# Down projection of a gated conv FFN on one core: where the raw weight rows of the seven-product units lie, which queue loads them, and how many such units there are

## The chip, the cores and the metric

The kernel runs on one core of one Trainium2 chip. The metric is the device time of one execution in microseconds (us). Each time given is a median of a few executions. The trace of before is one more execution of the same kernel, recorded by the hardware profiler.

## The reference

One decoder layer on 256 tokens with a model width of 2048: a mixer of two attention branches, then a gated feed-forward network. Only the last part of the second one matters here, the down projection of a [256, 5632] activation with a [5632, 2048] float32 matrix, followed by a norm with the scale `norm_ffn_post` and the residual sum.

```python
def conv_ffn(h, w_up, conv_w, conv_b, w_down):
    a, b = jnp.split(h @ w_up, 2, axis=-1)
    ...
    return (jax.nn.gelu(c, approximate=True) * b) @ w_down

h = rms_norm(x, norm_ffn_pre[l])
y = conv_ffn(h, ffn_w_up[l], ffn_conv_w[l], ffn_conv_b[l], ffn_w_down[l])
x = x + rms_norm(y, norm_ffn_post[l])
```

## The kernel before

All weights are float32 in DRAM. A chunk of 128 rows by 1024 columns (512 KB) comes into a **raw** tile. ScalarE rounds it to a high half `whi`, VectorE subtracts to get the low half `wlo` (`convert`, lines 143 and 144), and TensorE multiplies in three passes (`mm3`, lines 175 to 177: high weights, low weights, then high weights with the low half of the activation). The raw tiles are a ring of three (`RAW = 3`), the pairs of halves a ring of four and one more; a load is issued on SyncE's queue as soon as its raw tile has been read by both engines, and SyncE takes its loads strictly in order.

The 5632 columns of the activation are made in eleven groups of 512 (`ffn_up(c, ...)`, c = 0 to 10, lines 1041 and 1045). Each group leaves two evacuation tiles, tags `fa` and `fb` with two buffers each, which the convolution and the gating (`conv_cols`, lines 930 to 938) read. After group 5 the first 24 tiles of 128 columns (k = 0 to 23) are complete, and `down_pair(p)` multiplies them with their rows of `w_down`: p = 0 for output columns 0 to 1023, p = 1 for columns 1024 to 2047. Then come groups 6 to 10 and the rest of the down projection.

`down_pair` walks over 12 **units** of two row tiles each, of two kinds:

- `plain(u)`: two rows of weights through SyncE and the raw ring, each multiplied with both token tiles and both halves of the columns, 2 x 4 products of three passes: 24 matmuls.
- `seven(u)`: the two rows `even` and `odd` and the two token tiles are taken as a 2 x 2 block product, done with seven products instead of eight: 21 matmuls. VectorE forms four sums of weights (`ta`, `tb`, lines 1124 to 1127, in tiles of the tags `fa` and `fb`); `odd`, half of `even`, `ta` and `tb` are converted, in this order. The sums of the activation (`s_of`) were made earlier, for units 0 to 3.

In the text a unit of seven products is called a seven, and the sevens are numbered through both passes. `PAIR_ORDER` writes out the order of the units: `psppsppsppsp`, the same for both p, so there are 2 x 4 sevens and 2 x 8 plain units. The products use all eight PSUM banks, four named `c` and four named `q`; the two sets change places between p = 0 and p = 1. After the last seven of a pass VectorE and ScalarE empty `q` into `ds` (lines 1141 to 1145), after the last unit `c` (line 1155). After p = 1 the next group's product `ua` writes into the banks that were `q`.

`gpost2` is the tile with the scale `norm_ffn_post`, 1 MB for 128 partitions. It uses the one buffer of tag `gp`, is loaded on GpSimd's queue before group 1, and is read first after group 10. Between, GpSimd's queue only writes the residual stream to DRAM (`park`, line 1007). It is read back on SyncE's queue (`unpark`, line 1013) into tiles that the token sums `s` hold before.

Inside `trunk_layer` a scheduler puts the instructions of each engine into a fixed order when the program is built; each engine then runs its list in that order and waits on semaphores.

Of the kernel before, what the change touches and what calls it, by code (L numbers as in the profile page):

```python
# [19 lines left out]
P = 128  # L20
D = 2048
# [20 lines left out]
def trunk_layer(ctx, tc, x, x_cols_in, conv_cols_in, g_mix_post, g_ffn_post, w_in, w_q, w_kv,  # L42
                sinks, rel, wo_a, wo_b, w_out, w_up, w_down, rope_tab, strip_sel, out):
    nc = tc.nc
    vec, act, pe, pool = nc.vector, nc.scalar, nc.tensor, nc.gpsimd

    def open_pool(name, bufs=1, **kw):
        es = ExitStack()
        return es, es.enter_context(tc.tile_pool(name=name, bufs=bufs, **kw))
# [9 lines left out]
    def sb(pl, shape, name, dt=F32, tag=None, bufs=None):  # L59
        return pl.tile(shape, dt, name=name, tag=tag or name, **({"bufs": bufs} if bufs else {}))  # L60
# [46 lines left out]
    def ring_tile(kind, name, dt, extra):  # L107
        pl_tag = dict(name=name, tag="flex", bufs=2) if extra else dict(name=name, tag=kind, bufs=RAW if kind == "raw" else RING)
        return ring.tile([P, 1024], dt, **pl_tag)

    def in_turn(kind):

        turn[kind] += 1
        return flex[0] == kind and turn[kind] % (RAW + 2 if kind == "raw" else RING + 1) >= (RAW if kind == "raw" else RING)
# [19 lines left out]
    def convert(raw, n, own=None, parts=None):  # L134
        i = cnt[0]
        cnt[0] += 1
        if own:
            hi, lo = (own.tile([P, 1024], F32R, name=f"w{part}{i}", tag="w" + part) for part in ("hi", "lo"))
        else:
            extra = in_turn("w")  # L140
            hi, lo = (ring_tile("w" + part, f"w{part}{i}", F32R, extra) for part in ("hi", "lo"))
        for a, b in parts or ((0, n),):
            act.copy(hi[:, a:b], raw[:, a:b])  # L143
            vec.tensor_tensor(lo[:, a:b], raw[:, a:b], hi[:, a:b].bitcast(F32), op=ALU.subtract)  # L144
        return hi, lo

    def raw_row(src):
        i = cnt[0]
        cnt[0] += 1
        raw = ring_tile("raw", f"raw{i}", F32, in_turn("raw"))  # L150
        nc.sync.dma_start(raw, src)
        return raw
# [4 lines left out]
    def at(t, *fs):  # L157
        steps[max(t, now[0])].extend(fs)

    def tick():  # L160
        for f in steps.pop(now[0], ()):
            f()
        now[0] += 1
# [10 lines left out]
    def mm3(o, ah, al, bh, bl, start, stop):  # L174
        pe.matmul(o, ah, bh, start=start, stop=False)  # L175
        pe.matmul(o, ah, bl, start=False, stop=False)  # L176
        pe.matmul(o, al, bh, start=False, stop=stop)  # L177

    def gemm(xh, xl, w, k0, nk, c0, n, split=None, extra=None, ps=None):

        kc = 1024 // n if n in (256, 512) else 2
        acc = new_acc("g", ps)
        todo = []
        cuts = list(range(0, nk, kc)) + [nk]
        for ci, (k, ke) in enumerate(zip(cuts[:-1], cuts[1:])):
            kk = ke - k
            src = w[(k0 + k) * P:(k0 + k + kk) * P, c0:c0 + n].rearrange("(a p) n -> p a n", p=P)
            hi, lo = wchunk(src, [kk, n], *(extra or {}).get(ci, ()))
            for j in range(kk):
                kt = k + j  # L190
                wh, wl = hi[:, j * n:(j + 1) * n], lo[:, j * n:(j + 1) * n]
                for t in range(NT):
                    x_ = [x(k0 + kt)[:, t * P:(t + 1) * P] for x in (xh, xl)]
                    if split is None or t == 0 or ci < split:
                        mm3(acc[t][:, :n], *x_, wh, wl, kt == 0, kt == (split * kc if split and t else nk) - 1)
                    else:
                        todo.append((kt, x_, wh, wl))
            tick()
        return acc, todo
# [377 lines left out]
    acc, _ = gemm(XH, XL, w_in, 0, KT, 0, 512)  # L577
# [4 lines left out]
    acc, _ = gemm(XH, XL, w_in, 0, KT, C_KV, KVR + ROPE)  # L582
# [201 lines left out]
    for j in range(4):  # L784
        acc, _ = gemm(XH, XL, w_in, 0, KT, C_GA + 512 * j, 512)
# [15 lines left out]
    es6, p6 = open_pool("p6")  # L801
# [33 lines left out]
    for j in range(4):  # L835
        ld = merge_loads(j)
        acc, _ = gemm(AH, AL, wo_a, 0, KT, 512 * j, 512)
# [60 lines left out]
    for b in range(4):  # L898
        c0, n = W_BLOCKS[b]
# [109 lines left out]
    def unpark(t, j):  # L1009
        if j == 0:  # L1010
            x2_all[t] = sb(p3, [P, D], f"x2b_{t}", tag=f"x2_{t}")
        c = slice(j * 512, (j + 1) * 512)
        nc.sync.dma_start(x2_all[t][:, c], x2_d[t, :, c])
# [59 lines left out]
            at(now[0] + 1 + 2 * i, lambda i=i: conv_cols(4 * c + i, sa[0][i], sa[1][i], slot0 + i))  # L1073

    es7 = ffn_up0()
    gpost2 = sb(p6, [P, D], "gpost2", tag="gp")
    pool.dma_start(gpost2, g_ffn_post.partition_broadcast(P))
    for c in range(1, 6):
        if c == 2:
            for i in range(8):  # L1080
# [11 lines left out]
    def banks(kind, name):  # L1092
        return [(pacc if kind == 0 else (pss, pst)[i // 2]).tile([P, 512], F32, name=f"{name}{i}", tag="acc" if kind == 0 else "st"[i // 2])
                for i in range(4)]

    def down_pair(p):

        c11, c12, c21, c22 = c = banks(p, f"c{p}_")
        q1, q5, q7, q6 = q = banks(1 - p, f"q{p}_")
        j0, used = 2 * p, set()  # L1100
        d = [dsum[t][j0 + j] for t in range(NT) for j in range(2)]
        act_of = lambda k, t: (GH(k)[:, t * P:(t + 1) * P], GL(k)[:, t * P:(t + 1) * P])
        row = lambda k: w_down[k * P:(k + 1) * P, j0 * 512:(j0 + 2) * 512]
        half = lambda w, i: tuple(x[:, i * 512:(i + 1) * 512] for x in w)

        def mul(o, x, w, last=False):
            mm3(o, *x, *w, id(o) not in used, last)
            used.add(id(o))

        def plain(u, last):  # L1110
            for k in (2 * u, 2 * u + 1):
                w = convert(raw_row(row(k)), 1024)
                for t in range(NT):
                    for j in range(2):
                        mul(c[2 * t + j], act_of(k, t), half(w, j), last and k % 2 == 1)
                tick()

        def seven(u, last):
            s1, s2, s3, s4 = s_of[u]
            even, odd = raw_row(row(2 * u)), raw_row(row(2 * u + 1))  # L1120
            ta, tb = (sb(p6, [P, 1024], f"t{n}{p}_{u}", tag="f" + n, bufs=2) for n in "ab")
            lo_, hi_ = slice(0, 512), slice(512, 1024)
            w = convert(odd, 1024)
            vec.tensor_tensor(ta[:, lo_], even[:, hi_], even[:, lo_], op=ALU.subtract)
            vec.tensor_tensor(ta[:, hi_], odd[:, hi_], even[:, hi_], op=ALU.subtract)
            vec.tensor_tensor(tb[:, lo_], odd[:, hi_], ta[:, lo_], op=ALU.subtract)
            vec.tensor_tensor(tb[:, hi_], odd[:, lo_], tb[:, lo_], op=ALU.subtract)
            mul(c11, act_of(2 * u + 1, 0), half(w, 0))
            mul(c12, s4, half(w, 1))
            w = convert(even, 512)  # L1130
            mul(q1, act_of(2 * u, 0), half(w, 0), last)
            w = convert(ta, 1024)
            mul(q5, s1, half(w, 0), last)
            mul(q7, s3, half(w, 1), last)
            tick()
            w = convert(tb, 1024)
            mul(q6, s2, half(w, 0), last)
            mul(c21, act_of(2 * u + 1, 1), half(w, 1))
            tick()
            if last:  # L1140
                act.copy(d[0], q1)
                vec.tensor_tensor(d[1], d[0], q6, op=ALU.add)
                vec.tensor_tensor(d[2], d[1], q7, op=ALU.add)
                vec.tensor_tensor(d[3], d[2], q5, op=ALU.add)
                vec.tensor_tensor(d[1], d[1], q5, op=ALU.add)  # L1145

        plain_of, seven_of = iter(range(4, 12)), iter(range(4))
        for i, kind in enumerate(PAIR_ORDER):
            if kind == "s":
                u = next(seven_of)  # L1150
                seven(u, u == 3)
            else:
                plain(next(plain_of), i == len(PAIR_ORDER) - 1)
        for o, x in zip(d, c):
            vec.tensor_tensor(o, o, x, op=ALU.add)

    for p in range(2):
        down_pair(p)
    for i in range(8):
        at(now[0] + 40 + 2 * i, lambda i=i: unpark(i // 4, i % 4))  # L1160
    for c in range(6, 11):
# [65 lines left out]


RING = 4
PAIR_ORDER = "psppsppsppsp"  # L1230
XCUT = [0, 1, 2, 3, 4, 6, 8, 10, 12, 14, 16]
X_LOAD = [0, 1, 2, 3, 4, 6, 7, 8, 10]
X_SQ = [4, 4, 5, 5, 6, 7, 8, 9, 10, 11]
# [71 lines left out]
```

## Time and profile before

| what | value |
|---|---|
| median of 3 runs | 1474.38 us (1473.21 to 1476.98) |
| the profiled execution | 1475.35 us |
| its span, from the first to the last instruction | 1473.5 us |
| TensorE busy | 1460.6 us, 99% of the span |
| VectorE, ScalarE busy | 1026.6 us (70%), 818.3 us (56%) |
| GpSimd busy | 51.1 us (3%) |
| DMA | 287.58 MB, 195 GB/s in the mean |

The profiled execution is 0.97 us above the median, and 1.85 us of it lie outside the span. In a row of the timeline the first number is the start in us from the span's begin, the second the time from the first start to the last end of the instructions merged in the row; a bracket at the end says how long the engine was idle before and who released it. Matmuls are pipelined, so a matmul's own 0.39 us is longer than the time from one to the next.

### The profile page before, as it was taken

The page shows a single profiled execution, that of the slowest core. Times are in us where ns is not written, and L with a number is a line of the kernel's source. Part 1 is how long each engine was busy: PE and PEld are TensorE (multiplying, and loading weights), DVE is VectorE, ACT ScalarE, POOL GpSimd, SP SyncE. Part 2 cuts the span into 40 slices and gives each one's busy share as a digit, 9 for nine tenths or more (in the row PEclk, how much of TensorE's full clock was granted, in tenths as well). Part 3 has the DMA queues.
Part 4 walks back from the last instruction along what each step waited for, and adds up shares of the span by engine and source line. Part 5 has one row for each costly group of instructions (what it writes and reads, how often), then busy time and mean ns, then how long its engine had stood idle before and what let it go on. Part 6 is the DMA issues. An engine that isn't in the chain of part 4 may idle for free.

```text
span 1473.5 us, 20861 instructions
## 1 busy us (share of the span) xinstructions
PE 1460.6 (99%) x7591; PEld 1246.1 (85%) x7591; DVE 1026.6 (70%) x1799; ACT 818.3 (56%) x1354; POOL 51.1 (3%) x87
## 2 busy tenths in 40 slices
PE   9999999999999999999999999999999999999997
PEld 7888888888888888888888888888877888888886
DVE  7788874445667665555799877677777676677556
ACT  7588864444565554444666565555444565565443
POOL 0021100000000010000000000000000000000000
PEclk9999999999999999999999999999999999999999
DMA  8755376666655559755766666665667666666653
GB/s 291 223 171 165 94 219 195 206 209 200 186 160 156 171 163 339 224 197 195 224 202 184 192 193 185 188 196 162 209 199 226 210 200 190 194 186 187 198 189 126
DMA packets 154513, 287.58 MB, mean 195 GB/s; under 512 B 18427, under 2 KB 29596, under 8 KB 154284
## 3 DMA queue, kind: packets, MB, share of 16 engines
q1 hardware_dynamic: 149664, 270.43, 59.4%
q0 software_dynamic: 4656, 15.78, 3.4%
q8 instruction: 59, 0.97, 0.3%
q14 instruction: 42, 0.34, 0.1%
q10 hardware_dynamic: 92, 0.05, 0.0%
HBM read 277.79 MB, written 8.44 MB: 194 GB/s over the span
## 4 chain that ended last, share of the span: by engine, by line
PE 92%; DVE 3%; DMA 3%; ACT 1%; issue 0%; DVEq 0%; ACTq 0%; SPq 0%
PE accg L175 15%; PE accg L177 15%; PE accg L176 15%; PE ub L1041 10%; PE ua L1041 10%; PE ua L1045 5%; PE ub L1045 5%; DMA raw<-in_ffn_w_down_dram 2%; PE c L175 1%; PE c L176 1%; PE c L177 1%; DVE wlo L144 1%; PE mpo L760 1%; PE ms L726 1%; PE pt L442 1%; PE qn L691 1%
## 5 line engine op out<-in xcount | busy, mean ns | idle before, releaser
L144 DVE TENSOR_TENSOR wlo<-raw,whi 128x1024 fp32r<-128x1024 f32 (+2 forms) x502 | 604.7, 1207 | 345.4 <-ACT whi L143 340.6
L143 ACT CAST whi<-raw 128x1024 fp32r<-128x1024 f32 (+2 forms) x502 | 518.6, 1036 | 495.7 <-PE accg L177 239.2
L175 PE MATMUL accg<-whi,ahl 128*128 128x512 f32 (+1 forms) x544 | 212.9, 391 | 0.0
L177 PE MATMUL accg<-whi,ahl 128*128 128x512 f32 (+1 forms) x544 | 210.5, 387 | 0.0
L176 PE MATMUL accg<-wlo,ahl 128*128 128x512 f32 (+1 forms) x544 | 209.7, 385 | 0.0
L175 PE MATMUL accg<-whi,bhl 128*128 128x512 f32 x442 | 173.0, 391 | 0.0
L177 PE MATMUL accg<-whi,bhl 128*128 128x512 f32 x442 | 172.3, 390 | 0.0
L176 PE MATMUL accg<-wlo,bhl 128*128 128x512 f32 x442 | 172.2, 390 | 0.0
L1041 PE MATMUL ua<-ahl,whi 128*128 128x512 f32 x640 | 154.8, 391 | 0.9 <-DVE ds L1145 0.9
L1041 PE MATMUL ub<-ahl,whi 128*128 128x512 f32 x640 | 154.6, 391 | 0.0
L1041 PEld LDWEIGHTS ua<-ahl,whi 128*128 128x128 f32 x640 | 117.4, 188 | 24.0 <-DVE ds L1145 1.3
L1041 PEld LDWEIGHTS ub<-ahl,whi 128*128 128x128 f32 x640 | 117.5, 188 | 22.9 <-ACT cc L930 0.3
L177 PEld LDWEIGHTS accg<-whi,ahl 128*128 128x128 f32 x544 | 102.1, 188 | 20.6
L176 PEld LDWEIGHTS accg<-wlo,ahl 128*128 128x128 f32 x544 | 102.3, 188 | 18.1
L175 PEld LDWEIGHTS accg<-whi,ahl 128*128 128x128 f32 x544 | 102.3, 188 | 17.9
L177 PEld LDWEIGHTS accg<-whi,bhl 128*128 128x128 f32 x442 | 83.0, 188 | 17.4
L175 PEld LDWEIGHTS accg<-whi,bhl 128*128 128x128 f32 x442 | 83.0, 188 | 16.9
L176 PEld LDWEIGHTS accg<-wlo,bhl 128*128 128x128 f32 x442 | 83.0, 188 | 16.8
L1045 PEld LDWEIGHTS ub<-ahl,wlo 128*128 128x128 f32 x640 | 82.2, 191 | 3.2
L1045 PEld LDWEIGHTS ua<-ahl,wlo 128*128 128x128 f32 x640 | 82.2, 191 | 3.1
L1045 PE MATMUL ua<-ahl,wlo 128*128 128x256 f32 x640 | 83.7, 283 | 0.0
L1045 PE MATMUL ub<-ahl,wlo 128*128 128x256 f32 x640 | 83.2, 283 | 0.0
(409 smaller groups left out, 1876.1 us busy)
## 6 DMA issues: line engine op xcount, KB each, us to landing
raw<-in_ffn_w_up_dram SPq DMA_DIRECT2D x176, 512.0 KB, 4.5
raw<-in_w_in_dram SPq DMA_DIRECT2D x111, 512.0 KB, 4.4
raw<-in_ffn_w_down_dram SPq DMA_DIRECT2D x88, 512.0 KB, 4.3
raw<-in_w_o_swa_dram SPq DMA_DIRECT2D x32, 512.0 KB, 4.3
raw<-in_w_o_mla_dram SPq DMA_DIRECT2D x32, 512.0 KB, 4.8
raw<-in_w_out_dram SPq DMA_DIRECT2D x32, 512.0 KB, 4.2
bias<-strip POOLq DMA_DIRECT2D x16, 256.0 KB, 4.3
raw<-in_mla_w_q_up_dram SPq DMA_DIRECT2D x32, 128.0 KB, 2.6
```

Of the source, the lines that this page charges most:

```text
L143: act.copy(hi[:, a:b], raw[:, a:b])
L144: vec.tensor_tensor(lo[:, a:b], raw[:, a:b], hi[:, a:b].bitcast(F32), op=ALU.subtract)
L175: pe.matmul(o, ah, bh, start=start, stop=False)
L176: pe.matmul(o, ah, bl, start=False, stop=False)
L177: pe.matmul(o, al, bh, start=False, stop=stop)
L442: pe.transpose(pt[:, j * P:(j + 1) * P], p[:, c * P:(c + 1) * P], ident)
L691: pe.matmul(o, wl, ch(k), start=False, stop=k == nk - 1)
L726: pe.matmul(o, w, v_, start=n == 0, stop=False)
L760: pe.matmul(o, w(t), p_[:, c], start=n == 0, stop=n == 5)
L1041: pe.matmul(acc[i], hi[:, c], hn[p][:, j * 512:(j + 1) * 512], start=p + j == 0, stop=stop)
L1045: pe.matmul(acc[i][:, 0:256], lo[:, c], hn[p][:, j * 512:j * 512 + 256], start=False, stop=False)
```

## The change

The rows of a seven no longer go through the raw ring and SyncE's queue. Odd-numbered sevens, counted over both passes, put them side by side into one tile of tag `gp`, where the scale lay; even-numbered ones put them into one tile each of the tags `fa` and `fb`. Both loads are issued on GpSimd's queue. The scale is loaded after both passes. In the second pass the order of the units is another, with three sevens instead of four.

```diff
     es7 = ffn_up0()
-    gpost2 = sb(p6, [P, D], "gpost2", tag="gp")
-    pool.dma_start(gpost2, g_ffn_post.partition_broadcast(P))
...
+    sevens_done = [0]
...
         def seven(u, last):
             s1, s2, s3, s4 = s_of[u]
-            even, odd = raw_row(row(2 * u)), raw_row(row(2 * u + 1))
+            sevens_done[0] += 1
+            if sevens_done[0] % 2:
+                both = sb(p6, [P, D], f"rr{p}_{u}", tag="gp")
+                even, odd = both[:, 0:1024], both[:, 1024:2048]
+            else:
+                even, odd = (sb(p6, [P, 1024], f"rr{p}_{u}{n}", tag="f" + n, bufs=2) for n in "ab")
+            pool.dma_start(even, row(2 * u))
+            pool.dma_start(odd, row(2 * u + 1))
             ta, tb = (sb(p6, [P, 1024], f"t{n}{p}_{u}", tag="f" + n, bufs=2) for n in "ab")
...
-        plain_of, seven_of = iter(range(4, 12)), iter(range(4))
-        for i, kind in enumerate(PAIR_ORDER):
+        sevens = PAIR_ORDER[p].count("s")
+        plain_of, seven_of = iter(range(sevens, 12)), iter(range(sevens))
+        for i, kind in enumerate(PAIR_ORDER[p]):
             if kind == "s":
                 u = next(seven_of)
-                seven(u, u == 3)
+                seven(u, u == sevens - 1)
...
     for p in range(2):
         down_pair(p)
+    gpost2 = sb(p6, [P, D], "gpost2", tag="gp")
+    pool.dma_start(gpost2, g_ffn_post.partition_broadcast(P))
...
-PAIR_ORDER = "psppsppsppsp"
+PAIR_ORDER = ("psppsppsppsp", "ppsppsppsppp")
```

GpSimd's list, behind the parking of the first half of the residual stream. A name `rr0_1b` is pass 0, unit 1, row `odd`; without a letter both rows lie in one tile.

```order
 L1007 DMA x2_d_2541<-x2_0_5774 128x512 x4
-L1077 DMA gpost2_7658<-in_norm_ffn_post_dram 128x2048
+L1126 DMA rr0_0_9946<-in_ffn_w_down_dram 128x1024
+L1127 DMA rr0_0_9946<-in_ffn_w_down_dram 128x1024
 L1007 DMA x2_d_2541<-x2_1_5775 128x512 x4
-L1300 UNCONDITIONAL_BRANCH
-L1300 ISA
+L1126 DMA rr0_1a_10103<-in_ffn_w_down_dram 128x1024
+L1126 DMA rr0_2_10222<-in_ffn_w_down_dram 128x1024
+L1127 DMA rr0_2_10222<-in_ffn_w_down_dram 128x1024
+L1127 DMA rr0_1b_10104<-in_ffn_w_down_dram 128x1024
+L1126 DMA rr0_3a_10340<-in_ffn_w_down_dram 128x1024
```

The two rows of L1300 are the program's end. The first seven's rows take the place of the scale. The second seven's `odd` row stands behind both rows of the third seven. Each of these loads waits for the last reader of the tile that it overwrites: `rr0_2` for the first seven's readers of `rr0_0`, `rr0_1b` for the conversion of the first seven's `tb`, in whose buffer it is put.

VectorE's list ahead of the second seven of pass 0, first before. `raw684` and `raw685` are the rows `even` and `odd` of that seven, `raw682` the last row of the plain units ahead of it, `uu23` the last gating of group 5.

```order
L144 TENSOR_TENSOR wlo681_10060<-raw680_10057,whi681_10059 128x1024
L937 TENSOR_SCALAR uu23_10094<-uu23_10094,cc23_10093 128x256
L938 TENSOR_TENSOR uu23_10094<-uu23_10094,f1_5_9882 128x256
L144 TENSOR_TENSOR wlo683_10078<-raw682_10075,whi683_10077 128x1024
L231 TENSOR_TENSOR ghl11_7475<-uu23_10094,ghl11_7475 128x256
L1124 TENSOR_TENSOR ta0_1_10110<-raw684_10106 128x512
L1125 TENSOR_TENSOR ta0_1_10110<-raw685_10108,raw684_10106 128x512
L1126 TENSOR_TENSOR tb0_1_10111<-raw685_10108,ta0_1_10110 128x512
L144 TENSOR_TENSOR wlo686_10113<-raw685_10108,whi686_10112 128x1024
```

The same place now; the last plain row is `raw680` here.

```order
L144 TENSOR_TENSOR wlo679_10057<-raw678_10054,whi679_10056 128x1024
L937 TENSOR_SCALAR uu23_10091<-uu23_10091,cc23_10090 128x256
L1132 TENSOR_TENSOR ta0_1_10107<-rr0_1b_10104,rr0_1a_10103 128x512
L938 TENSOR_TENSOR uu23_10091<-uu23_10091,f1_5_9880 128x256
L1133 TENSOR_TENSOR tb0_1_10108<-rr0_1b_10104,ta0_1_10107 128x512
L144 TENSOR_TENSOR wlo681_10075<-raw680_10072,whi681_10074 128x1024
L231 TENSOR_TENSOR ghl11_7475<-uu23_10091,ghl11_7475 128x256
L144 TENSOR_TENSOR wlo682_10110<-rr0_1b_10104,whi682_10109 128x1024
L1134 TENSOR_TENSOR tb0_1_10108<-rr0_1b_10104,tb0_1_10108 128x512
```

The sums that read the seven's own rows (now lines 1131 to 1134) have moved ahead of the low half of the last plain row.

VectorE's list at the end of pass 1, first before. `raw774` and `raw776` are the two rows of the last plain unit, `raw778` and `raw780` the first two chunks of `w_up` for group 6, and L1142 to L1145 empty the banks `q1`.

```order
L144 TENSOR_TENSOR wlo775_10892<-raw774_10889,whi775_10891 128x1024
L144 TENSOR_TENSOR wlo777_10910<-raw776_10907,whi777_10909 128x1024
L144 TENSOR_TENSOR wlo779_10936<-raw778_10933,whi779_10935 128x1024
L1142 TENSOR_TENSOR ds0_7476<-ds0_7476,q1_3_10443 128x512
L1143 TENSOR_TENSOR ds1_7477<-ds0_7476,q1_2_10442 128x512
L144 TENSOR_TENSOR wlo781_10958<-raw780_10955,whi781_10957 128x1024
L1144 TENSOR_TENSOR ds1_7477<-ds1_7477,q1_1_10441 128x512
L1145 TENSOR_TENSOR ds0_7476<-ds0_7476,q1_1_10441 128x512
L1155 TENSOR_TENSOR ds0_7476<-ds0_7476,c1_0_10436 128x512
```

The same place now, from the third of the last six plain rows (`raw754`) on; `raw762` to `raw766` are the first chunks for group 6.

```order
L144 TENSOR_TENSOR wlo755_10839<-raw754_10836,whi755_10838 128x1024
L1149 TENSOR_TENSOR ds0_7476<-ds0_7476,q1_3_10439 128x512
L1150 TENSOR_TENSOR ds1_7477<-ds0_7476,q1_2_10438 128x512
L1151 TENSOR_TENSOR ds1_7477<-ds1_7477,q1_1_10437 128x512
L1152 TENSOR_TENSOR ds0_7476<-ds0_7476,q1_1_10437 128x512
L144 TENSOR_TENSOR wlo757_10857<-raw756_10854,whi757_10856 128x1024
L144 TENSOR_TENSOR wlo759_10875<-raw758_10872,whi759_10874 128x1024
L144 TENSOR_TENSOR wlo761_10893<-raw760_10890,whi761_10892 128x1024
L144 TENSOR_TENSOR wlo763_10921<-raw762_10918,whi763_10920 128x1024
L144 TENSOR_TENSOR wlo765_10943<-raw764_10940,whi765_10942 128x1024
L144 TENSOR_TENSOR wlo767_10965<-raw766_10962,whi767_10964 128x1024
L1163 TENSOR_TENSOR ds0_7476<-ds0_7476,c1_0_10432 128x512
```

The emptying of `q1` stood behind the first chunk for group 6; it now stands three plain rows ahead of it.

More of the change, by code (lines that the diff above doesn't have):

```diff
@@ L1145, in seven @@
                 vec.tensor_tensor(d[1], d[1], q5, op=ALU.add)
-        plain_of, seven_of = iter(range(4, 12)), iter(range(4))
-        for i, kind in enumerate(PAIR_ORDER):
+        sevens = PAIR_ORDER[p].count("s")
+        plain_of, seven_of = iter(range(sevens, 12)), iter(range(sevens))
+        for i, kind in enumerate(PAIR_ORDER[p]):
             if kind == "s":
                 u = next(seven_of)
-                seven(u, u == 3)
+                seven(u, u == sevens - 1)
             else:
-                plain(next(plain_of), i == len(PAIR_ORDER) - 1)
+                plain(next(plain_of), i == len(PAIR_ORDER[p]) - 1)
         for o, x in zip(d, c):
```

## The prediction

> **What bounds the kernel now.** The page first: busy times, then the chain that ended last.
>
> ```profile
> PE 1460.6 (99%) x7591; PEld 1246.1 (85%) x7591; DVE 1026.6 (70%) x1799; ACT 818.3 (56%) x1354; POOL 51.1 (3%) x87
> PE 92%; DVE 3%; DMA 3%; ACT 1%; issue 0%; DVEq 0%; ACTq 0%; SPq 0%
> ```
>
> TensorE carries nearly all of the chain, so a gain can only come from matmuls that are dropped or from the few places where TensorE waits. The chain has 3% of DMA and 3% of VectorE in it, and the change touches one stretch, so I cut that stretch into the two passes of the down projection, the hand-over to group 6 and what follows (columns: window, its length, busy us and instructions of PE, PEld, DVE, ACT, POOL, then clock, DMA share, GB/s).
>
> ```profile
> 1003.91:1066.47 62.56, 62.56 (x278) 51.80 (x276) 50.04 (x63) 32.43 (x40) 0.00 (x0) 1.00 0.60 190
> 1066.47:1132.44 65.97, 64.16 (x277) 51.49 (x276) 48.15 (x54) 31.18 (x33) 0.00 (x0) 1.00 0.64 200
> 1132.44:1135.46 3.02, 2.10 (x10) 1.42 (x9) 3.02 (x6) 1.05 (x1) 0.00 (x0) 1.00 0.83 271
> 1135.46:1340.00 204.54, 204.54 (x1179) 180.87 (x1178) 144.51 (x232) 115.44 (x180) 0.00 (x0) 1.00 0.66 199
> ```
>
> Both passes issue the same 8 x 24 + 4 x 21 = 276 matmuls. Pass 0 takes 62.56 us for them and TensorE is busy in all of it: 62.56 / 276 = 0.2267 us from one matmul to the next is the pitch without a wait. Pass 1 takes 65.97 us, 3.41 us more. Most of the excess is at two sevens (TensorE's timeline):
>
> ```profile
> 1087.78 0.39 PE L177 MATMUL c<-whi,bhl 128*128 128x512 f32 x1
> 1088.19 0.50 PE L175 MATMUL c<-whi,bhl 128*128 128x512 f32 x1
> 1089.52 0.50 PE L176 MATMUL c<-wlo,bhl 128*128 128x512 f32 x1 [0.82 <-DVE wlo L144]
> 1120.71 0.50 PE L175 MATMUL c<-whi,bhl 128*128 128x512 f32 x1
> 1122.02 0.50 PE L176 MATMUL c<-wlo,bhl 128*128 128x512 f32 x1 [0.80 <-DVE wlo L144]
> 1132.44 0.84 PE L1041 MATMUL ua<-ahl,whi 128*128 128x512 f32 x3
> 1134.20 1.42 PE L1041 MATMUL ua<-ahl,whi 128*128 128x512 f32 x5 [0.92 <-DVE ds L1145]
> ```
>
> At 1088.19 and at 1120.71 the first high pass of a seven has started and the low pass waits for `wlo`; between their starts lie 1.33 and 1.31 us where 0.23 is the pitch. The last two rows are the hand-over: three matmuls of group 6 run, the next waits for the emptying of `q`. Its eight matmuls take 3.02 us, at the pitch 1.81, so 1.21 us are lost. The chain says what was late in each case:
>
> ```profile
> 1081.38 5.63 DMA raw<-in_ffn_w_down_dram
> 1087.03 0.69 DVE ta L1125
> 1087.72 0.60 DVE tb L1126
> 1088.32 1.14 DVE wlo L144
> 1113.51 6.00 DMA raw<-in_ffn_w_down_dram
> ...
> 1129.27 1.23 DVE wlo L144
> 1130.49 0.61 DVE ds L1142
> ...
> 1133.54 0.61 DVE ds L1145
> ```
>
> The seven's `odd` row was issued at 1081.38, landed 5.63 us later, and TensorE was there one microsecond after. The loads have no lead, because a seven holds two of the three raw tiles. At the end, the emptying of `q` is finished 1.1 us after pass 1, since only one plain unit follows its last seven. Of 69 us, then, 3.41 + 1.21 = **4.62 us** are waiting. The window after it has none: 204.54 busy of 204.54.
>
> **The change part by part.** *One seven fewer:* pass 1 issues 9 x 24 + 3 x 21 = 279 matmuls, three more: 3 x 0.2267 = **+0.68 us**, all on TensorE's path.
>
> *The sevens' rows leave the raw ring.* Plain units and sevens in the ratio 2 to 1 take (2 x 24 + 21) x 0.2267 = 15.64 us. In it SyncE's ring had to turn over six rows, one in 2.61 us; it now turns over four, one in 3.91 us. The cost of one turn:
>
> ```profile
> L144 DVE TENSOR_TENSOR wlo<-raw,whi 128x1024 fp32r<-128x1024 f32 x20 | 24.4, 1222 | 10.7 <-ACT whi L143 10.6
> L143 ACT CAST whi<-raw 128x1024 fp32r<-128x1024 f32 x20 | 20.9, 1050 | 29.3 <-DMA raw<-in_ffn_w_down_dram 28.0 <-DMA raw<-in_ffn_w_up_dram 1.1 <-PE c L177 0.2
> raw<-in_ffn_w_down_dram SPq DMA_DIRECT2D x42, 512.0 KB, 4.5
> ```
>
> 4.5 + 1.05 + 1.22 = 6.8 us, over three tiles 2.26 us per row. Before, that was barely enough with all three tiles going round and not enough with two of them held; now it leaves a third. ScalarE's 28.0 us of waiting for these rows should nearly vanish, and so should TensorE's 3.41 us, if the sevens' rows come in time from GpSimd. No GpSimd load of 512 KB is in the trace; the nearest rows are its loads and stores of 256 KB and its one load of 1 MB:
>
> ```profile
> bias<-strip POOLq DMA_DIRECT2D x16, 256.0 KB, 4.3
> x_d<-x POOLq DMA_DIRECT2D x8, 256.0 KB, 5.9
> gpost<-in_norm_ffn_post_dram POOLq DMA_DIRECT2D x1, 1024.0 KB, 4.8
> DMA to landing us min/median/max: 4.5/5.9/6.5
> ```
>
> (the last row is of the x_d stores). I take 5.9 us, the slower kind, and 6.5 as the upper end. The tightest case is the second seven. Its `odd` row overwrites the first seven's `tb`, read last by the conversion at 1007.96, and VectorE's other marks are (VectorE's timeline):
>
> ```profile
> 1005.51 0.68 DVE L1127 TENSOR_TENSOR tb<-raw,tb 128x512 f32<-128x512 f32 x1
> 1007.96 1.23 DVE L144 TENSOR_TENSOR wlo<-tb,whi 128x1024 fp32r<-128x1024 f32 x1 [0.29 <-ACT whi L143]
> 1015.17 0.42 DVE L938 TENSOR_TENSOR uu<-uu,f 128x256 f32<-128x256 f32 x1
> 1024.45 1.22 DVE L144 TENSOR_TENSOR wlo<-tb,whi 128x1024 fp32r<-128x1024 f32 x1
> ```
>
> So it is issued at 1009.2, behind the third seven's two rows, which are free at 1006.2, and lands at 1015.1 to 1015.7. On VectorE `ta` (L1132) now waits for it ahead of the low half of the last plain row, which TensorE wants after a plain unit, a seven and three rows: 1003.91 + (24 + 21 + 36) x 0.2267 = 1022.27. Between stand two sums of 0.69, 0.42 of gating and 1.22: the row must be there by 1019.2. A lead of 10.0 us against 5.9; queued behind that wait is all of VectorE's list, but it is 3.5 us early. The fourth seven's rows are free at 1025.7. VectorE reads them ahead of the low half of the third seven's `tb`, which TensorE wants after five plain units, two sevens and 15 matmuls, at 1044.0; less two sums of 0.69 and 1.22 that is 1041.4, a lead of 15.7. The third seven's rows are wanted in the same manner behind the second's `ta`, at 1025.1, and free at 1006.2: a lead of 18.9. In pass 1 the distances are the same or longer. I book **-3.41 us** for pass 1; pass 0 has nothing to gain. The range of this term is 0 to -3.41, and a loss only in the rival below.
>
> *Three plain units behind the last seven.* They give the emptying of `q` 72 x 0.2267 = 16.3 us instead of 5.4; it needs four sums of about 0.6, and stands ahead of three plain rows on VectorE. **-1.21 us** at the hand-over. Next late could be the first chunks of `w_up`; SyncE now issues the read-back of the second half of the residual ahead of them. That read waits for the last seven's token sums, 16 us before the hand-over, while the raw tile of the first chunk is free only when the fourth of the last six rows is converted. So it holds nothing up.
>
> *The scale's load moves* from the start of group 1 to the last third of pass 1, when the last seven's rows have been read. It is read only after group 10. Its 1 MB adds 3.9 us of transfer at the 271 GB/s of the hand-over's row, beside rows with slack: 0, at worst those 3.9 us. VectorE's sums have the same count per seven, and one seven fewer: off the path.
>
> Sum: -3.41 - 1.21 + 0.68 = **-3.94 us**. The profiled execution would go from 1475.35 to 1471.41; it lies 0.97 us above the median of the runs, so against that median 1474.38 - 3.94 = **1470.4 us**, 0.27% less. About 0.3% (4.4 us) is what a measurement of this kernel can tell from no change.
>
> **The rivals.** *Bytes, not tiles, are the limit.* If the transfers as a whole were too slow in pass 1, another queue would not help and the waits would stay: 1474.38 + 0.68 = 1475.1 us. For it: landings of 5.63 and 6.00 us at the two waits, over the 4.5 in the middle. Against it: pass 0 moved 190 GB/s without a wait, pass 1 200, and the hand-over's row 271, so there is room. The Trainium skill, DMA: Bandwidth & Descriptors, section "Issuing engines are not separate DMA queues", has the rule that stands behind it: loads issued from several engines run on the same 16 DMA engines and save only issue time. By that rule alone the change would bring its +0.68; the trace agrees about the bytes, but shows that it is the time of issue that was late. Chance 0.12.
>
> *The hand-over gets crowded.* The scale, the read-back, the last plain rows and the first chunks of `w_up` meet from 1105 on, and up to 3.9 us come back as waits: 1470.4 to 1474.3 us. For it, the 0.83 DMA share at 1132; against it, the three plain rows converted ahead. Chance 0.10.
>
> *GpSimd's loads come late because VectorE keeps it from preparing them.* VectorE is busy for 48.15 of the 65.97 us of pass 1. If GpSimd could only work in the rest, 5.9 us would become 5.9 x 65.97 / 17.82 = 21.8 us. With landings of 20 us the second seven loses 20 - 10.0, the fourth 20 - 15.7, the third 20 - 18.9: 15.4 us, so 1474.38 - 3.94 + 15.4 = 1485.8 us, slower. It makes the kernel more than 0.3% slower where landings pass 17 us (2 x 17 - 25.7 = 8.3 eats the 3.94 and 4.4 more). Against it stand the 16 bias loads: they landed in 4.3 us, between 40.8 and 167.7 us of the span, where VectorE was busy for 7 to 8 tenths (its busy tenths in 40 slices of 36.8 us; the loads lie in the second to the fifth):
>
> ```profile
> DVE  7788874445667665555799877677777676677556
> L453 POOL DMA_DIRECT2D bias<-strip x16: 722/722/746, 40.8 to 167.7; - x16
> ```
>
> The Trainium skill, SBUF — State Buffer, section "SBUF: two separate sides", warns of this trap: a VectorE operation in a two-port mode keeps GpSimd from writing its descriptors. By the same page's section "Who interferes with whom" the form that fills this stretch, tensor_tensor, has no such mode, and would cost nothing; no row here shows the two-port case. Chance 0.08.
>
> **How the numbers follow.** The forecast has the remaining 0.70. It lies 0.5 us above the 0.3% line at 1469.96, and single runs of before differ by 3.8 us, so about 0.3 of the 0.70 falls below the line: faster 0.30. The first two rivals and the rest of the forecast are no change: 0.62. Slower is the third: 0.08. The range reaches from 1.4 us below the forecast (the lowest run was 1.2 below its median) to the crowded hand-over, with the scatter 1474.5 us; it leaves out the slow rival and most of the unchanged one.
>
> **What would show it.** Right: pass 1 takes 279 x 0.2267 = 63.2 us, group 6 starts at about 1129.7 without a bracket, ScalarE's waits for `w_down` rows fall from 52 us in the two passes to under 15, GpSimd's loads land in 5 to 7 us. Wrong: a bracket at the second or fourth seven behind a sum that reads `rr`, landings over 10 us, or waits at 1113 to 1130. The 52 us are this row of the waits from 1003 to 1137:
>
> ```profile
> ACT whi L143 <- DMA raw<-in_ffn_w_down_dram: 52.2, 27, 5.5
> ```

## The result, and the profile after

The changed kernel takes 1471.77 us (median of 16 executions, 1470.95 to 1472.41), the kernel before, run beside it, 1474.64 us (16 executions, 1473.21 to 1476.98). The ratio is 0.998, with an interval of 0.9972 to 0.9987: 2.87 us less, where 3.94 were forecast. The profiled execution took 1471.75 us with a span of 1470.0. The spread of the single times has shrunk too, from 3.8 to 1.5 us.

The busy times of the page after, and behind them the four windows (the two passes, the hand-over, what follows; columns as in the prediction):

```profile
PE 1460.2 (99%) x7594; PEld 1247.9 (85%) x7594; DVE 1023.2 (70%) x1793; ACT 818.1 (56%) x1352; POOL 58.6 (4%) x101
```

```profile
1004.49:1067.05 62.56, 62.56 (x278) 51.80 (x276) 52.71 (x68) 33.66 (x42) 4.75 (x9) 1.00 0.61 202
1067.05:1130.30 63.25, 63.25 (x281) 52.38 (x280) 45.34 (x47) 29.81 (x31) 1.58 (x3) 1.00 0.66 220
1130.30:1132.11 1.81, 1.81 (x10) 1.50 (x9) 0.58 (x1) 1.10 (x2) 0.00 (x0) 1.00 0.78 247
1132.11:1336.60 204.49, 204.49 (x1179) 180.82 (x1178) 144.01 (x232) 113.90 (x179) 0.00 (x0) 1.00 0.65 192
```

TensorE is busy in the whole of every window. Pass 1 takes 63.25 us, 279 x 0.2267, and the hand-over 1.81. Both passes and the hand-over together, called **the stretch** below, are 62.56 + 63.25 + 1.81 = 127.62 us (127.61 by the starts of the matmuls, before rounding). Before they were 62.56 + 65.97 + 3.02 = 131.55: between the two profiled executions the 3.94 us of the forecast are gone. The window behind holds the same 1179 matmuls in both, and TensorE is busy in all of it.

GpSimd's loads and VectorE's use of the tightest one (DMA issues with the median us to landing; then timelines of GpSimd and VectorE, start and duration first):

```profile
rr<-in_ffn_w_down_dram POOLq DMA_DIRECT2D x8, 512.0 KB, 5.4
rr_1b<-in_ffn_w_down_dram POOLq DMA_DIRECT2D x2, 512.0 KB, 4.8
rr_3a<-in_ffn_w_down_dram POOLq DMA_DIRECT2D x1, 512.0 KB, 4.1
```

```profile
1010.06 0.53 POOL L1127 DMA_DIRECT2D rr_1b<-in_ffn_w_down_dram  x1 [1.67 <-DVE wlo L144]
1015.95 0.68 DVE L1132 TENSOR_TENSOR ta<-rr_1b,rr_1a 128x512 f32<-128x512 f32 x1
```

The second seven's `odd` row is issued at 1010.06 and read by VectorE at 1015.95 without a bracket, that is, without a wait. ScalarE and GpSimd wait as follows in 1000 to 1135 us (us in total, times, longest):

```profile
ACT whi L143 <- DMA raw<-in_ffn_w_down_dram: 18.8, 10, 3.4
ACT whi L143 <- PE c L177: 30.7, 24, 2.1
POOL gpost L1168 <- DVE wlo L144: 29.0, 1, 29.0
```

ScalarE now waits mostly for TensorE (`PE c`), which means that it has run ahead; its waits for rows fell from 52.2 to 18.8 us.

### The profile page after: what moved, and what is told of

Same layout as the page of the kernel before. It is cut to its first block, busy times and chain, and to the rows that moved or that the text cites. A ratio compares the mean times of both kernels' runs of the same rounds, so it can differ in the third digit from the quotient of the medians.

```text
span 1470.0 us, 20862 instructions
## 1 busy us (share of the span) xinstructions
PE 1460.2 (99%) x7594; PEld 1247.9 (85%) x7594; DVE 1023.2 (70%) x1793; ACT 818.1 (56%) x1352; POOL 58.6 (4%) x101
## 4 chain that ended last, share of the span: by engine, by line
PE 96%; DVE 2%; ACT 1%; issue 1%; DVEq 0%
PE accg L175 15%; PE accg L177 15%; PE accg L176 15%; PE ub L1041 10%; PE ua L1041 10%; PE ub L1045 5%; PE ua L1045 5%; PE c L176 2%; PE c L175 2%; PE c L177 2%; PE mpo L760 1%; PE ms L726 1%; PE qn L689 1%; PE qn L691 1%; PE qn L690 1%
## 5 line engine op out<-in xcount | busy, mean ns | idle before, releaser
L144 DVE TENSOR_TENSOR wlo<-raw,whi 128x1024 fp32r<-128x1024 f32 (+2 forms) x488 | 591.9, 1216 | 347.2 <-ACT whi L143 342.4
L143 ACT CAST whi<-raw 128x1024 fp32r<-128x1024 f32 (+2 forms) x488 | 507.9, 1043 | 469.8 <-PE accg L177 246.3
```

## Experiments

All times of before in these comparisons lie between 1474.28 and 1474.67 us (medians of 16 to 27 executions beside each on the same chip). "Waiting" is the stretch less what its matmuls take at the pitch, with 1.81 for the hand-over: 126.93 us for eight sevens, 127.61 for seven, 126.25 for nine, 125.57 for ten.

A stretch is read from one execution, a median from several. Outside the stretch the fourteen profiled executions take 1343.4 to 1345.4 us, so the times of two single executions can differ by 2 us at the same stretch. The order alone, the tiles and queue alone, the loads on SyncE and the eight sevens were timed together, beside the same 27 executions of before; so were the two variants of before, beside 19.

| kernel | median us (executions) | ratio, interval | stretch of the profiled execution | waiting in it |
|---|---|---|---|---|
| before | 1474.64 (16) | 1 | 131.55, again 129.89 and 129.24 | 4.62, 2.96, 2.31 |
| after | 1471.77 (16) | 0.998, 0.9972 to 0.9987 | 127.61, again 127.61 | 0 |
| order alone | 1472.3 (11) | 0.9983, 0.9974 to 0.9992 | 127.61 | 0 |
| tiles and queue alone | 1471.68 (8) | 0.9975, 0.9965 to 0.9985 | 126.93 | 0 |
| after, loads on SyncE | 1472.3 (11) | 0.9984, 0.9975 to 0.9992 | 127.61 | 0 |
| after, one tile | 1480.33 (5) | 1.004, 1.0027 to 1.0053 | 133.72 | 6.11 |
| after, eight sevens | 1471.54 (8) | 0.9977, 0.9966 to 0.9987 | 126.93 | 0 |
| before, last seven dropped | 1472.7 (10) | 0.9987, 0.9978 to 0.9996 | 128.14 | 0.53 |
| before, a plain unit more at the border | 1473.05 (10) | 0.999, 0.9981 to 1.0 | 127.65 | 0.72 |
| nine sevens | 1471.05 (11) | 0.9978, 0.9969 to 0.9987 | 126.25 | 0 |
| ten sevens | 1470.9 (11) | 0.9979, 0.9971 to 0.9988 | 126.60 | 1.03 |

**The two halves apart.** First the order of the units alone: before, rows through the raw ring and SyncE, the scale loaded early. The loop that takes an order for each pass is as in the change; it is left out here and in the two other variants of before.

```diff
...
-PAIR_ORDER = "psppsppsppsp"
+PAIR_ORDER = ("psppsppsppsp", "ppsppsppsppp")
```

> The new order with three sevens in the second pass; the rows of the sevens still go through the raw ring and SyncE's queue, and the scale is loaded early. Theory (two separate causes: the ring's three tiles cost the waits inside the second pass, the short tail behind the last seven costs the wait at the hand-over): three matmuls more, +0.68 us, no wait at the hand-over, -1.21 us, and waits inside the second pass still there, 1 to 3 us: about 1473 to 1474 us, more than 1 us above the change. Rival (the order alone brings the gain): as fast as the change, 1471.8 us, and no wait inside the second pass.

Measured 1472.3 us and, in the profiled execution, no wait at all: the theory of two separate causes fails. Windows of the two passes and of the hand-over, and the first of ScalarE's waits:

```profile
1004.25:1130.05 125.80, 125.80 (x557) 104.17 (x556) 96.72 (x113) 63.77 (x72) 0.00 (x0) 1.00 0.66 212
1130.05:1131.86 1.81, 1.81 (x10) 1.50 (x8) 1.25 (x2) 0.76 (x1) 0.00 (x0) 1.00 0.87 259
```

```profile
ACT whi L143 <- DMA raw<-in_ffn_w_down_dram: 39.8, 25, 3.3
```

ScalarE still waits 39.8 us for rows, against 52.2 before, and TensorE for nothing. So waits of ScalarE are no measure of what the ring costs, and in this execution the three raw tiles do suffice for seven sevens. Then the other half, the changed kernel with the old order:

```diff
-PAIR_ORDER = ("psppsppsppsp", "ppsppsppsppp")
+PAIR_ORDER = ("psppsppsppsp", "psppsppsppsp")
```

> The new tiles and queue, but the old order with four sevens in both passes. Theory: no waits inside the second pass, so 62.56 us for it, and a wait of about 1.2 us at the hand-over as before: 0.5 us above the change, 1472.3 us (three matmuls less, 1.2 us of waiting more). Rival (the tiles give nothing without the longer tail and the order): within 1 us of before, 1474.6 us.

Measured 1471.68 us, again without a wait, also at the hand-over, where 1.2 us were expected although one plain unit follows the last seven as before. VectorE's emptying of `q` and the first matmuls of group 6, here (the first three rows) and in a second profile of before (the last three; it has other line numbers for the same sums):

```profile
1123.74 0.68 DVE L1149 TENSOR_TENSOR ds<-ds,q 128x512 f32<-128x512 f32 x1
1127.46 0.68 DVE L1152 TENSOR_TENSOR ds<-ds,q 128x512 f32<-128x512 f32 x1
1128.68 1.98 PE L1041 MATMUL ua<-ahl,whi 128*128 128x512 f32 x8
```

```profile
1129.66 0.68 DVE L1142 TENSOR_TENSOR ds<-ds,q 128x512 f32<-128x512 f32 x1
1132.71 0.68 DVE L1145 TENSOR_TENSOR ds<-ds,q 128x512 f32<-128x512 f32 x1
1131.61 0.84 PE L1041 MATMUL ua<-ahl,whi 128*128 128x512 f32 x3
```

With the new tiles the first of the four sums starts 4.9 us ahead of group 6 and the last ends 0.54 us ahead of it. In before the first starts 1.95 us ahead and the last ends 1.78 us behind the start. The plain unit after the last seven is the same in both, and so is the order of VectorE's list there. What differs is how late VectorE is when it comes to the sums. In this profile of before it has waited for both raw rows of the last seven, 2.92 us together:

```profile
1116.13 0.69 DVE L1124 TENSOR_TENSOR ta<-raw 128x512 f32<-128x512 f32 x1 [1.03 <-DMA raw<-in_ffn_w_down_dram]
1118.71 0.69 DVE L1125 TENSOR_TENSOR ta<-raw,raw 128x512 f32<-128x512 f32 x1 [1.89 <-DMA raw<-in_ffn_w_down_dram]
```

With the new tiles VectorE's sums wait for no row in the two passes. Either half alone therefore removes the waits from the profiled execution, and the two gains do not add.

**Queue or tiles.** The changed kernel, the sevens' loads issued by SyncE:

```diff
-            pool.dma_start(even, row(2 * u))
-            pool.dma_start(odd, row(2 * u + 1))
+            nc.sync.dma_start(even, row(2 * u))
+            nc.sync.dma_start(odd, row(2 * u + 1))
```

> The change with one thing undone: the two rows of each seven are loaded on SyncE's queue, into the same tiles, in the order of the units. Theory (tiles are what was short, not the queue): the rows still come more than 5 us early, so no wait inside the second pass, within 0.3 us of the change, 1471.8 us. Rival (SyncE's strict order is what was late; a load that waits for its tile holds the plain rows behind it): waits of 1 us or more at several units, 1473 us or more.

The stretch is 127.61 us, the loads into `rr` land in 4.7 us in the middle instead of 5.4, and nothing waits, as the theory said. In the profile GpSimd's queue brings nothing of its own. That agrees with the Trainium skill, DMA: Bandwidth & Descriptors, section "Issuing engines are not separate DMA queues". The median lies 0.5 us above that of the changed kernel. It is that of the order alone, though, and the two kernels with eight sevens timed beside both lie 0.6 and 0.8 us below, where three matmuls fewer make 0.68. So a hidden wait is not needed to explain this median; what sets the changed kernel's 0.5 us lower is not shown.

**How much lead.** The changed kernel with all sevens in the one tile of the scale:

```diff
-            if sevens_done[0] % 2:
+            if True:
```

> The changed kernel with the raw rows of all its sevens in the one tile of the scale, so that a seven's loads wait until the seven before it has read that tile: less lead, and the evacuation tiles hold only sums. Theory 'any tiles outside the three raw ones, with a lead of one unit, are enough' (loads land in 5.4 us, at most 6.5; between two sevens lie two plain units of 5.4 us): no wait, two passes and hand-over 127.61 us, 1471.8. Rival 'the two-unit lead by turns is needed': a part of the waits comes back, 128.5 us or more, 1472.7 and up.

The theory was wrong, and the rival holds by far more than it asked for: 1480.33 us, 6.05 us slower than before. Timelines of GpSimd, VectorE and TensorE around the first large wait, and VectorE's and GpSimd's waits in 1000 to 1140 us:

```profile
1035.71 0.68 DVE L144 TENSOR_TENSOR wlo<-rr,whi 128x512 fp32r<-128x512 f32 x1
1036.68 0.53 POOL L1126 DMA_DIRECT2D rr<-in_ffn_w_down_dram  x1 [13.18 <-DVE wlo L144]
1042.20 0.69 DVE L1131 TENSOR_TENSOR ta<-rr 128x512 f32<-128x512 f32 x1 [4.28 <-DMA rr<-in_ffn_w_down_dram]
1042.81 1.22 DVE L144 TENSOR_TENSOR wlo<-tb,whi 128x1024 fp32r<-128x1024 f32 x1
1045.87 2.35 DVE L144 TENSOR_TENSOR wlo<-raw,whi 128x1024 fp32r<-128x1024 f32 x2
1047.14 0.50 PE L176 MATMUL c<-wlo,ghl 128*128 128x512 f32 x1 [1.15 <-DVE wlo L144]
```

```profile
POOL rr L1126 <- DVE wlo L144: 82.6, 5, 21.5
DVE ta L1131 <- DMA rr<-in_ffn_w_down_dram: 16.1, 6, 4.3
```

The tile is free at 1036.4, when VectorE has converted the `even` row of the seven before. Its list has the next seven's first sum almost at once, behind one more conversion. So the landing of 5.5 us is not covered by the two plain units that TensorE computes in between: VectorE works that far ahead of TensorE. It stands still for 4.28 us, with the previous seven's `wlo<-tb` and the plain rows' low halves queued behind it, and TensorE waits for those. What TensorE loses is what VectorE's head start does not cover: VectorE's six waits for rows are 16.1 us in all, TensorE's waiting is 6.11. The lead of a row counts from the last read of its tile to its place in VectorE's list, and only the work that VectorE has done ahead stands between a wait there and TensorE.

**Border and tail.** Two variants of before (rows through the raw ring) tell where the old order was tight. In the first the last seven of the second pass is left out, in the second one more plain unit stands between the first pass and the first seven, and the number of sevens stays eight.

```diff
...
-PAIR_ORDER = "psppsppsppsp"
+PAIR_ORDER = ("psppsppsppsp", "psppsppspppp")
```

> Before, with rows still through the three raw tiles and SyncE's queue, but three sevens in the second pass in place of four: the last seven of the tail is left out, and the pass begins as in before (p s p p s). Theory 'the border of the passes': the wait comes from raw rows and conversions that fall behind where VectorE empties the sums of the first pass and a seven follows after one plain unit; then the waits at 1076 to 1090 us (about 1.6 us) stay, and those of the tail with the hand-over (1.3 and 1.2 us) go: two passes and hand-over about 129 us, 1473. Rival 'number of sevens': any one seven fewer is enough, no wait at all: 127.6 us, 1472.0.

```diff
...
-PAIR_ORDER = "psppsppsppsp"
+PAIR_ORDER = ("psppsppsppsp", "ppspsppsppsp")
```

> Before, rows still through the three raw tiles, four sevens in both passes, but the second pass begins p p s p s, so that a plain unit more stands between the border of the passes and the first seven, and two sevens stand only one plain unit apart after it. Theory 'the border': the first waits (1076 to 1090 us) go, and with them what follows from being late; at most the tail's remain: two passes and hand-over 127 to 129.3 us, 1471.3 to 1473. Rival 'number of sevens' (the ring can't bring eight sevens' rows): waits of 3 to 4.6 us as in before, 1474.6.

The first has 0.53 us of waiting left, at the first sevens of the pass, and none in the tail. The second has none in the pass and 0.72 at the hand-over. Windows of the second, and its hand-over:

```profile
1004.38:1129.50 125.12, 125.12 (x553) 103.60 (x552) 98.50 (x117) 63.72 (x73) 0.00 (x0) 1.00 0.64 201
1129.50:1132.03 2.53, 2.11 (x9) 1.42 (x8) 2.53 (x6) 1.05 (x1) 0.00 (x0) 1.00 0.93 297
```

```profile
1130.04 0.68 DVE L1145 TENSOR_TENSOR ds<-ds,q 128x512 f32<-128x512 f32 x1
1130.77 1.43 PE L1041 MATMUL ua<-ahl,whi 128*128 128x512 f32 x5 [0.42 <-DVE ds L1145]
```

Eight sevens go through the raw ring in 125.12 us, at the pitch: in this execution three tiles bring the rows in time for TensorE. VectorE's sums (`ta`) wait 11.2 us for rows in it and 11.7 in the first profile of before; here VectorE's head start covers all of that in the passes. It was a good execution, 1471.91 us, the second fastest of ten. By the two stretches this variant should be 0.49 us faster than the first, and its median is 0.35 us slower, so other executions seem to wait longer; no trace shows where. Each place costs by itself, and in these two profiles each goes by itself. The forecast of 1.6 us left at the border in the first variant was too much; the next two profiles of before vary there too.

**Before and after once more.** The kernels unchanged, for further profiles.

> The kernel before once more, unchanged, for a second profile of it: the waits of the two passes and of the hand-over. Theory A (the waits differ from execution to execution): two passes and hand-over other than 131.55 us by some tenths or more, nearer 130.5 to 131.2. Theory B (the waits are the same each time, and the smaller median gain comes from the start-up): 131.5 to 131.6 again.

> The changed kernel once more, unchanged, for a second profile: two passes and hand-over 127.61 us as before, since nothing waits there; the first sum of products' start between 56.5 and 57.8 us, other than 57.30 (scatter of the start-up).

> The kernel before a third time, for the scatter of its waits: two passes and hand-over were 131.55 and 129.89 us in two profiles. If the waits differ from execution to execution, a third value between 129 and 132; that they sit at other matmuls than before is expected too.

The windows of before, second profile (three rows: pass 0, pass 1, hand-over) and third:

```profile
1004.82:1067.50 62.68, 62.68 (x278) 51.94 (x277) 50.87 (x65) 32.52 (x40) 0.00 (x0) 1.00 0.61 191
1067.50:1131.61 64.11, 63.70 (x277) 51.30 (x276) 47.45 (x53) 31.20 (x33) 0.00 (x0) 1.00 0.65 204
1131.61:1134.71 3.10, 2.11 (x9) 1.42 (x8) 3.10 (x6) 1.05 (x1) 0.00 (x0) 1.00 0.86 261
```

```profile
1067.50:1130.90 63.40, 63.40 (x278) 51.56 (x276) 47.72 (x54) 31.20 (x33) 0.00 (x0) 1.00 0.65 207
1130.90:1134.16 3.26, 2.10 (x9) 1.42 (x8) 3.26 (x6) 1.05 (x1) 0.00 (x0) 1.00 0.85 244
```

The cut between the passes at 1067.50 is some tenths late, so the passes are taken together: less 125.12 us, they wait 1.67 us in the second profile and 0.86 in the third, against 3.41 in the first. The hand-over waits 1.29 and 1.45 us, against 1.21. So theory A holds, with stretches below the values that it named. The changed kernel's stretch is 127.61 us both times.

**More sevens.** With the new tiles nothing waits at eight sevens, so there is room. The changed kernel with one more in the tail:

```diff
-PAIR_ORDER = ("psppsppsppsp", "ppsppsppsppp")
+PAIR_ORDER = ("psppsppsppsp", "pspsppsppspp")
```

> The new tiles and queue, four sevens in the second pass again, but in the order pspsppsppspp, so that two plain units follow the last one. Theory: no wait anywhere, and three matmuls less than the change: 0.68 us below the change, 1471.1 us, the second pass at 62.56 us. Rival (the third seven less is needed, because sevens two units apart leave the conversions behind, or two plain units are too short a tail): a wait of 0.7 us or more, at the second pass's second seven or at the hand-over, and 1471.8 us or more.

Its profiled execution has no wait, as the theory said, and a stretch of 126.93 us; the median is 1471.54 us.

Then nine, as below, and ten with `pspspspspspp` in both passes. The activation's sums of a fifth pair are made in group 5; the lines that choose their tiles are left out:

```diff
...
+        if c == 5:
+            at(now[0] + 2, lambda: token_sums(4))
...
-PAIR_ORDER = ("psppsppsppsp", "ppsppsppsppp")
+PAIR_ORDER = ("psppsppsppsp", "pspspspspspp")
```

> The changed kernel with nine sevens: four in the first pass as now, five in the second (p s p s p s p s p s p p), the token sums of a fifth pair of rows made in group 5 in tiles that are free by then. A seven is three matmuls fewer: against the changed kernel's seven sevens, 6 x 0.2267 = 1.36 us less, two passes and hand-over 126.25 us if nothing waits: 1470.4. VectorE in the second pass: with four sevens 48.56 us of 62.60, one more adds 4.7: 53.2 of 61.9. Rival 'VectorE can't follow sevens one plain unit apart' (a seven with a plain unit takes 9.5 us of VectorE and 10.2 of TensorE, and the emptying of the first pass's eight sums, 5.5 us, comes at its start): a wait of 1 to 4 us, 1471.8 or above.

> The same with five sevens in both passes. 9 x 0.2267 = 2.04 us less than the changed kernel if nothing waits: two passes and hand-over 125.57 us, 1469.7. VectorE in the first pass: 52.7 us with four sevens, so 57.4 of 61.9 with five: theory 'full, with waits': 0.5 to 3 us of waits in the first pass, 1470.2 to 1472.7.

Windows of nine and of ten (passes), and ten's one wait of TensorE's matmuls in 1004 to 1131 us:

```profile
1005.33:1129.77 124.44, 124.44 (x550) 103.08 (x549) 105.43 (x126) 66.64 (x76) 8.43 (x16) 1.00 0.64 213
```

```profile
1004.65:1129.44 124.79, 124.09 (x547) 102.40 (x546) 109.98 (x132) 68.62 (x78) 9.50 (x18) 1.00 0.65 212
```

```profile
PE q L176 <- DVE wlo L144: 0.7, 1, 0.7
```

Nine sevens run at the pitch, with the 126.25 us expected. Ten save three matmuls more and lose 1.03 us, nearly all at 1025 us, where the end of group 5's gating and two sevens close together keep VectorE busy without a pause (1019.8 to 1027 us). That is within the 0.5 to 3 us expected. The medians of 1471.54, 1471.05 and 1470.9 us lie 0.2 to 0.9 us under the changed kernel's, in the direction of the counts, but the intervals against before overlap: a version that is clearly better than the changed kernel is not shown.

## Why the prediction was right, and where not

- **The pitch, and the waits as the only thing to win:** right. Every profiled execution without a wait follows the pitch of 0.2267 us: 127.61 us for seven sevens, 126.93 for eight, 126.25 for nine.
- **+0.68 us for one seven fewer:** right. It is the difference of the changed kernel with seven and with eight sevens, 127.61 - 126.93.
- **-3.41 us for pass 1:** the term that was mis-sized. It was read from one execution of before, and this wait changes from one to the next: 3.41, 1.67, 0.86 us. The stretch of before is 130.23 us in the mean of the three profiles, so the expected gain is 130.23 - 127.61 = 2.62 us; 2.87 were measured between the medians. The prediction put the profiled execution beside the median (0.97 us above it), but took off its waits in full.
- **The cause given for it, a ring too small for sevens:** only half right. The late rows were the thing that TensorE waited for at last, but the ring is at its edge, not plainly beyond it: in one execution with the sevens moved away from the border it brought eight without a wait in the pass, and in one with the new order alone seven. That it does so every time is not shown, and the medians speak against it for eight. The step that failed is "not enough with two of them held"; the working of 2.26 us per row against 2.61 had itself said that it was enough.
- **-1.21 us for the hand-over:** right in size (1.21, 1.29, 1.45 us before, 0 after), half right in its cause. "Since only one plain unit follows its last seven" is not enough, as the old order with the new tiles has no wait. The wait needs both, a short tail and a VectorE that comes late to the last seven's sums; three plain units cure it in one way and early rows in the other.
- **The scale's load at no cost:** the load took 8.2 us and waited 29.0 us in GpSimd's queue; nothing waits behind it in either window.
- **GpSimd's landings:** 5.9 us with 6.5 as the upper end were taken. The rows in `rr` landed in 3.7 to 6.5 us, 5.4 in the middle. The issue of the tightest row was read rightly too: 1010.06 (1009.2 forecast, in an execution that starts its passes 0.58 us later), and no wait. But its lead was counted to TensorE's need, 10.0 us; VectorE read it 5.89 us after its issue, 1.17 us after its landing of 4.72 us. A landing later than that would have held up VectorE first.
- **ScalarE's waits under 15 us:** missed, 18.8 us. The sign holds and it does not matter; 39.8 us of them cost nothing in the order alone.
- **0.3% as the least that can be told from no change:** too coarse. With 16 executions on each side the interval of the ratio, 0.9972 to 0.9987, leaves out 1.
- **Bytes as the limit:** refuted. Pass 1 moves 220 GB/s without a wait, where it moved 200 with 3.41 us of them.
- **A crowded hand-over:** refuted, 1.81 us at 247 GB/s.
- **GpSimd held up by VectorE:** its cause is refuted by the landings, in passes in which VectorE is busy for 52.71 of 62.56 and 45.34 of 63.25 us. That agrees with the Trainium skill, SBUF — State Buffer, section "Who interferes with whom", by which tensor_tensor has no two-port mode. But the consequence that the rival named is real: where a seven's rows come late, VectorE stands still and the plain rows behind it too. The lead that one tile leaves is short enough for that, without any delay of GpSimd's: 6.11 us of waiting in the profiled execution, 1480.33 us in the median.

What stays open: the median with one tile lies 2.8 us above its own profiled execution, and the variant with a plain unit more at the border 1.1 us. Whether that is the same change of waits from one execution to another was not tried, nor what makes before's waits vary.

## What to carry to other kernels

Count the lead of a prefetched tile from the read that frees it to the place of its first reader in that engine's own list, since an engine that works ahead of the bottleneck needs its data earlier than the bottleneck does; its head start decides how much of a wait reaches the bottleneck. A wait that sits on the edge differs from execution to execution: profile the kernel before two or three times ahead of booking such a wait as a gain. Where two edits cure the same lateness, their gains don't add, and the cheaper one (here the order, or the tiles without the other queue) may do by itself.

## What the hardware showed beside

The raw ring's waits vary by 2.3 us between executions of one program at the same granted clock (1.00 in all windows), and with them the time: 3.8 us from the fastest to the slowest of 16 executions of before, 1.5 to 2.2 us in the kernels whose profile shows no wait. The start-up varies as well. The first transposition of the attention's queries (L432) starts between 56.49 and 57.81 us in the fourteen profiles, ahead of all changed code, and the passes begin between 1003.56 and 1005.33 us. So two kernels that differ by less than a microsecond are told apart by their windows better than by their medians.
